# Moving the transposed activations of a two-layer decoder trunk to addresses that are multiples of 128 bytes

## The chip, the cores and the metric

The kernel runs on one core of one Trainium2 chip. The metric is the device time of one execution in microseconds (us). The kernel before took 676.93 us in the median of three runs (676.45 to 677.07).

## The reference

A causal decoder trunk of two layers over 256 tokens of 1024 features, all in float32. Each layer is a token mixer, a squared-ReLU MLP and a gated embedding; a final norm ends it.

```
u = rms_norm(h, attn_norm[i])
h = h + mixer_i(u)              # layer 0: 8 stick-breaking heads beside 4 differential heads
                                # layer 1: 16 heads of block attention (one block of 256 keys: causal softmax)
h = h + square(relu(rms_norm(h, mlp_norm[i]) @ w_ff1[i])) @ w_ff2[i]      # 1024 -> 4096 -> 1024
gate = sigmoid(rms_norm(h, ple_norm[i]) @ ple_gate[i])                    # 1024 -> 1024
h = h + gate * (p[i] @ ple_proj[i])                                       # 256 -> 1024
...
return rms_norm(h, final_norm)
```

The mixers project 1024 to 3072 features and the concatenated heads 1024 back to 1024.

## The kernel before

**Arithmetic.** To keep float32 accuracy at the speed of the one-pass format (float32r), each operand is split exactly into a high and a low part of that format, and each product is three matmuls into one bank of PSUM: high times high, high times low, low times high (`mm3`, and the same written out in `chunk_T` and `ff1`).

**Weights.** They stream from HBM in units of half a megabyte. A unit lands in one of four `raw` tiles; ScalarE writes its high part (`whi`, line 178) and VectorE the low part (`wlo`, line 192) into one of six pairs. TensorE releases a pair after its last product.

**Activations.** `transposes` turns the residual `h` with TensorE (line 170), ScalarE multiplies by the norm's gain from `gT`, and both parts go to one of two sets of transposed activations in turn: `T0h`/`T0l` and `T1h`/`T1l`, each tile [128, 8, 256] float32r, 8192 bytes in a partition. `Acts` hands the sets out by turns, so that the in-projections and the MLP's first product of both layers read `T0`, and the output projection of the mixer and the gate read `T1`. Attention results are written into `T1` by `average` and `put_T`.

**Which operand is which.** A matmul has a stationary operand, loaded into the array by LDWEIGHTS, and a moving one. The trace names them as bank<-moving,stationary. There are three kinds:
- `chunk`, `out_proj` and `gate`: 128 tokens of `T0` or `T1` are stationary, 512 columns of weights move (`bank<-whi,T0h` and so on). Only the last quarter of the last gate is cut to two pieces of 256 columns.
- `chunk_T` (line 574) and `ff1` (line 969): 128 columns of weights are stationary, 256 tokens of `T0` move (`bank<-T0h,whi`).
- `ff2` (line 993): 128 tokens of `hid`, the MLP's inner tile, are stationary, 512 columns of weights move (`bank<-whi,hid`). `hid` is a tile [128, 2, 4, 256] of the pool `zpool` (two buffers, shared with the attention's `z`), written by `hidden`.

All matmuls of these kinds are issued by line 159.

**Order of the work.** Tasks are Python generators with ranks; a list scheduler with its own clock estimates decides the order in which instructions are issued, once, at build time. It knows nothing of addresses. The feed-forward alternates `ff1(c + 1)` and `ff2(c)` over eight blocks of 512 inner features: 96 matmuls of 256 columns, then 48 of 512. Query and key projections leave `chunk` as a task that ScalarE scales, GpSimd rotates (`tt_pool`, line 196) and TensorE transposes; meanwhile TensorE goes on with the next products.

**Where tiles lie.** A pool places its tiles one behind the other in the order of their first allocation, each rounded up to 32 bytes; a tile of a name already allocated takes that name's place again. The pools `cst`, `zpool` and `vpool` follow one another. `cst` begins on a multiple of 128. Its large tiles are multiples of 128 bytes long; the small ones ahead of the transposed sets are these (`make_identity`'s tile is 512 bytes):

```
pexp = cst.tile([P, 2], F32, name="pexp")          # 8 bytes, takes 32
one = cst.tile([P, 1], F32, name="one")            # 4 bytes, takes 32
posi = cst.tile([P, 2], I32, name="posi")          # 8 bytes, takes 32
invf = cst.tile([P, 8], F32, name="invf")          # 32 bytes
gT = cst.tile([P, 48], F32, name="gT")             # 192 bytes
tsets = [[cst.tile([P, 8, 256], F32R, name=f"T{s}{w}") for w in ("h", "l")] for s in range(2)]
cc = cst.tile([P, 2, 2, 8], F32, name="cc")        # 128 bytes, and sn the same
```

In the program's list of addresses `whi0` is at byte 32896 of a partition (257 times 128; the other `whi` and `wlo` follow at steps of 4096), `T0h` at 131776 (1029 times 128, plus 64), `T0l`, `T1h` and `T1l` at steps of 8192 behind it, `pT` at 165856 (plus 96), and the two buffers of `hid` at 196224 and 204416 (1533 and 1597 times 128). All slices that the matmuls take of these tiles begin at multiples of 512 bytes in their tile.

Of the kernel before, what the change touches and what calls it, by code (L numbers as in the profile page):

```python
# [9 lines left out]
F32 = mybir.dt.float32  # L10
F32R = mybir.dt.float32r
# [6 lines left out]
P = 128  # L18
# [28 lines left out]

# ---- order of issue: tasks are generators that yield what they wait for; the one of the
# highest rank whose wait is over by the clocks of the engines issues next ----
class Event:  # L50
# [4 lines left out]
class Buffers:  # L55
    """Buffers that tasks take and give back."""

# [25 lines left out]
class Order:  # L83
# [65 lines left out]

    # -- instructions, each returning when its result can be read --  # L150
    def mm(self, out, lhsT, rhs, start, stop, **kw):
# [10 lines left out]
    def mm_halves(self, steps):  # L162
        """(out, lhsT, rhs, start, stop), 64 columns of the array each, two at a time side by side"""
        for out, lhsT, rhs, start, stop in steps:
            self.nc.tensor.matmul(out, lhsT, rhs, start=start, stop=stop)  # L165
            e = self.spend("pe", 0.84 * width(rhs) + 33)
        return e
# [13 lines left out]
    def after(self, out, *ins):  # L181
        """when the engine's own results are there"""
        w = 0.0
        for i in ins:
            if not isinstance(i, (int, float)) and i is not None:
                w = max(w, self.vis.get(i.tensor.name, 0.0))
        self.mine = out.tensor.name
        return w
# [24 lines left out]
    def copy(self, out, in_, ps=False, scale=None, dep=0.0):  # L213
        """On the engine that is through with it first."""
        n = width(out)
        ptr = scale is not None and not isinstance(scale, (int, float))
        ca = (52 if ps else 94) + 0.833 * n + (93 if ptr else 0)
        cv = 65 + (65 if ptr else 0) + (1.04 if ps else 0.52) * n
        if max(self.now, self.clk["act"], dep) + ca <= max(self.now, self.clk["dve"], dep) + cv:
            return self.act(out, in_, AF.Copy, ps=ps, dep=dep, scale=1.0 if scale is None else scale)  # L220
        if scale is None:
            self.nc.vector.tensor_copy(out, in_)
            return self.spend("dve", cv, dep)
        return self.ts(out, in_, scale, None, dep=dep, ps=ps)
# [3 lines left out]
def kernel(  # L228
# [7 lines left out]
    cst = ctx.enter_context(tc.tile_pool(name="cst", bufs=1))  # L236
# [5 lines left out]
    o = Order(nc)  # L242
# [14 lines left out]

# [1 line left out]
    h = [cst.tile([P, D], F32, name=f"h{t}") for t in range(2)]  # L259
# [34 lines left out]
    def constants_task():  # L294
# [4 lines left out]
        nc.gpsimd.memset(cmask, 0.0)  # L299
        # rows are queries, columns keys: a key after its query is out  # L300
        nc.gpsimd.affine_select(out=cmask[:, P:], in_=cmask[:, P:], pattern=[[-1, P]], base=0,
# [3 lines left out]
        for j in range(2):  # L305
            # rows are keys, columns queries: only keys before the query stay
            nc.gpsimd.affine_select(out=smask[:, j, :], in_=smask[:, j, :], pattern=[[1, P]], base=0,
                                    channel_multiplier=-1, compare_op=ALU.is_gt, fill=NEG)
        # negl[j, s] = -1 where j >= s
        nc.gpsimd.affine_select(out=neg[:, 0], in_=neg[:, 0], pattern=[[-1, P]], base=0,  # L310
# [17 lines left out]

    gT = cst.tile([P, 48], F32, name="gT")
    gT_ev = Event()  # L330
# [11 lines left out]

    o.add(gain_task(grow_a, 0, 16, 2800.0, gT_ev), 0)
    o.add(gain_task(grow_b, 16, 32, small_ev, Event()), 40)

# [1 line left out]
    specs = []  # L347
# [32 lines left out]
    units = []  # L380
# [33 lines left out]
    def short(eng, n):  # L414
        """at once when fewer than n units are ready, else when the engine is idle"""
        return lambda: o.now if ready[0] - used[0] < n else o.clk[eng]
# [41 lines left out]

# [1 line left out]
    tsets = [[cst.tile([P, 8, 256], F32R, name=f"T{s}{w}") for w in ("h", "l")] for s in range(2)]  # L460
    tnext = [0]
# [6 lines left out]

# [1 line left out]
    class Norm:  # L470
        """rs = 1/rms, rs8 = rs/8, rs2 = 1/rms^2 of each token tile"""

# [9 lines left out]
    def transposes(nm, t, c, dep, calm=False):  # L482
        """h[t][:, c] -> acts"""
        yield dep
# [27 lines left out]
    def statistics(nm, t, pieces, need):  # L512
        """pieces of the row: (first column, columns, event)"""
        for i, (c0, n, ev) in enumerate(pieces):
# [21 lines left out]

# [1 line left out]
    def mm3(ps, ahi, alo, whi, wlo, start, stop):  # L538
# [4 lines left out]
    def chunk(acts, sink, tmajor=False):  # L543
        """512 output features, token-major; sink(t, bank) is a task"""
        us = [take() for _ in range(4)]
# [28 lines left out]
    def chunk_T(acts, sink):  # L574
        """512 output features on partitions, 128 at a time; sink(f2, bank) is a task for two such blocks"""
        us = [take() for _ in range(4)]
# [15 lines left out]

# [1 line left out]
    cc = cst.tile([P, 2, 2, 8], F32, name="cc")  # L594
    sn = cst.tile([P, 2, 2, 8], F32, name="sn")
    rope_ev = Event()
# [42 lines left out]
    def rows_task(nm):  # L639
        """1/rms of each token along the columns, on every partition"""  # L640
        yield (nm.ev[0], nm.ev[1])
# [39 lines left out]
    def average(w0, w1, v, c0, acts, j, buf):  # L681
        """sum over keys of weights times values, for two heads of 64 features; w0(head) are the weights
        of the first 128 keys for all queries, w1(head) those of the last 128 for the last 128"""
        yield lambda: banks.wake(side=True)
# [12 lines left out]
    def put_T(oo, dep, acts, j):  # L697
        """token-major oo [128, 2 x 128] -> 128 features of acts"""
        yield dep
# [11 lines left out]

# [1 line left out]
    scores = [0, None]  # L713

    def scored():
        """a pair's scores are out"""
        scores[0] -= 1
        if scores[0] == 0:
            scores[1].t = o.now
# [45 lines left out]

# [1 line left out]
    def soft(j, t, qT, kz, q_ev, k_ev, e, st):  # L767
        """e [128, 2, (t+1)*128]; st: a column each for -max (2), sums (2), 1/sums (2)"""
        n = (t + 1) * P
# [9 lines left out]
        for g in range(2):  # L779
            # e = -(scores + mask), and its minimum is -max  # L780
            nc.vector.tensor_tensor_reduce(e[:, g, :], s3[:, g, :], cmask[:, P * (1 - t):], -1.0, 3.0e38, ALU.add, ALU.min,
                                           accum_out=st[:, g:g + 1])
            w = o.spend("dve", 130 + 1.04 * n)
# [63 lines left out]
    def moba_pair(j, jj, qT, kz, q_ev, k_ev, v, v_ev, acts):  # L847
        """heads 2*jj, 2*jj+1; j is the pair's place in its group"""
        yield (q_ev[0], k_ev[0], lambda: big.wake(2), lambda: tinies.wake(2))
# [25 lines left out]

# [1 line left out]
    def residual(t, c, bk, dep, scale, nm, h_ev):  # L877
# [186 lines left out]
    def finish(t, nm, gB, pieces):  # L1064
        """(h * gain) / rms, out"""
        parts = []
# [9 lines left out]

# [1 line left out]
    def table_task():  # L1078
# [12 lines left out]
        for t in range(2):  # L1091
            nc.gpsimd.tensor_tensor(ang[:, t, :], invf, posf[:, t:t + 1].to_broadcast([P, 8]), op=ALU.mult)  # L1092
        # ang = (ka 2^14 + kb) 2 pi + rem, with parts of 2 pi short enough that each product is exact
        magic, inv, b14 = 1.5 * 2.0 ** 23, 1.0 / (2.0 * math.pi), 2.0 ** 14
# [21 lines left out]
        yield e  # L1116
        # half angles: sin r = 2 sin(r/2) cos(r/2), cos r = 1 - 2 sin(r/2)^2
        o.act(sh, rem, AF.Sin, scale=0.5)
# [15 lines left out]
        rope_ev.t = e  # L1134
        # lambda of the differential heads, on every partition
        yield (28000.0, small_ev)
# [16 lines left out]
    o.add(table_task(), 15)  # L1153

    pT = cst.tile([P, 2, 2, 256], F32R, name="pT")

# [21 lines left out]
    def z_tile(name, layer, j):  # L1178
        """[128 features of two heads, pair, head, 256 tokens]; the other head's rows stay zero"""
        z = zpool.tile([P, 4, 2, 256], F32R, tag="z", name=name)  # L1180
# [11 lines left out]

# [1 line left out]
    def trunk():  # L1194
# [92 lines left out]
```

## Time and profile before

| | |
|---|---|
| median of three runs | 676.93 us (676.45 to 677.07) |
| profiled execution, first to last instruction | 674.7 us |
| TensorE matmul | 656.8 us busy, 97%, 3906 instructions |
| weight load (LDWEIGHTS) | 569.6 us, 84% |
| VectorE | 451.6 us, 67% |
| ScalarE | 417.1 us, 62% |
| GpSimd | 61.9 us, 9% |
| granted TensorE clock | 0.998 of full speed |
| DMA | 115.61 MB, 171 GB/s in the mean |

The profiled execution has a span of 674.7 us; the runs' median of 676.93 us has 2.2 us around such a span. Matmuls are pipelined: the recorded duration of one is longer than the distance from its start to the next one's start. That distance (the pitch below) is what the time is made of when TensorE never stops, and it is read from the starts in the timeline.

### The profile page before, as it was taken

What the parts mean: (1) busy time and instruction counts of PE and PEld (TensorE: products, weight loads), DVE (VectorE), ACT (ScalarE), POOL (GpSimd) and SP (SyncE); (2) the same over time, 40 slices, a digit from 0 to 9 for tenths busy, and PEclk for the clock granted to TensorE, in tenths of its full rate; (3) what the DMA queues carried; (4) which work ended last, traced back from release to release, by engine and by line L of the source; (5) the groups of instructions that cost most, each with busy time, mean ns of one, the idle gap of its engine ahead of it and who ended that gap; (6) DMA issues with size and microseconds to landing.
All of it is one profiled execution on the core that took longest, in us unless ns stands there. A gap on an engine that the chain in (4) does not pass through costs nothing.

```text
span 674.7 us, 10997 instructions
## 1 busy us (share of the span) xinstructions
PE 656.8 (97%) x3906; PEld 569.6 (84%) x3906; DVE 451.6 (67%) x936; ACT 417.1 (62%) x886; POOL 61.9 (9%) x129
## 2 busy tenths in 40 slices
PE   6799999999999999999999999999999999999995
PEld 4589878899998999898887777778998999899885
DVE  6789767777456554666895776758657545655584
ACT  7667887675446553655796776758646544655482
POOL 8820001000000000000043022000000000000010
PEclk9999999999999999999999999999999999999999
DMA  7753643456466546754656434435476546654621
GB/s 256 219 202 93 199 130 114 133 170 227 150 223 218 169 153 210 229 173 140 198 184 197 139 113 145 156 94 176 146 242 207 167 149 226 219 169 150 211 95 62
DMA packets 50054, 115.61 MB, mean 171 GB/s; under 512 B 4000, under 2 KB 5456, under 8 KB 50000
## 3 DMA queue, kind: packets, MB, share of 16 engines
q1 hardware_dynamic: 49824, 114.39, 52.0%
q8 instruction: 30, 0.49, 0.3%
q0 software_dynamic: 176, 0.53, 0.3%
q14 instruction: 24, 0.20, 0.1%
HBM read 113.86 MB, written 1.05 MB: 170 GB/s over the span
## 4 chain that ended last, share of the span: by engine, by line
PE 83%; issue 8%; POOL 7%; ACT 0%; DVE 0%; POOLq 0%; DVEq 0%; ACTq 0%
PE bank L159 80%; POOL rp L196 3%; PE bank L170 2%; PE bank L165 1%; POOL tok L196 1%; POOL prod L1102 1%; POOL rem L1103 1%; ACT tok L178 0%; POOL zl L1184 0%; POOL z L1185 0%; POOL z L1184 0%; POOL zl L1185 0%; POOL ang L1092 0%; POOL rs_a L527 0%; POOL rs_f L527 0%
## 5 line engine op out<-in xcount | busy, mean ns | idle before, releaser
L192 DVE TENSOR_TENSOR wlo<-raw,whi 128x512 fp32r<-128x512 f32 x424 | 276.9, 696 | 89.1 <-ACT whi L178 63.5
L178 ACT ACTIVATE whi<-raw 128x512 fp32r<-128x512 f32 x424 | 243.7, 628 | 97.9 <-PE bank L159 71.9
L159 PE MATMUL bank<-T0h,whi 128*128 128x256 f32 x576 | 161.7, 281 | 0.0
L159 PE MATMUL bank<-whi,hid 128*128 128x512 f32 x512 | 161.4, 391 | 0.0
L159 PE MATMUL bank<-T0l,whi 128*128 128x256 f32 x576 | 160.8, 279 | 0.0
L159 PE MATMUL bank<-T0h,wlo 128*128 128x256 f32 x576 | 160.7, 279 | 0.0
L159 PEld LDWEIGHTS bank<-whi,hid 128*128 128x128 f32 x512 | 96.1, 188 | 19.7
L159 PEld LDWEIGHTS bank<-T0h,whi 128*128 128x128 f32 x576 | 108.2, 188 | 0.7
L159 PEld LDWEIGHTS bank<-T0l,whi 128*128 128x128 f32 x576 | 107.8, 187 | 0.7
L159 PEld LDWEIGHTS bank<-T0h,wlo 128*128 128x128 f32 x576 | 108.2, 188 | 0.0
L159 PE MATMUL bank<-wlo,hid 128*128 128x512 f32 x256 | 99.6, 389 | 0.0
L192 DVE TENSOR_TENSOR tok<-tok 128x512 f32<-128x512 f32 x32 | 22.1, 690 | 67.1 <-ACT tok L178 67.1
L159 PE MATMUL bank<-whi,T0h 128*128 128x512 f32 x160 | 66.1, 413 | 0.2
L159 PE MATMUL bank<-wlo,T0h 128*128 128x512 f32 x160 | 63.7, 398 | 0.5 <-DVE wlo L192 0.4
L159 PE MATMUL bank<-whi,T0l 128*128 128x512 f32 x160 | 63.4, 396 | 0.0
L178 ACT ACTIVATE tok<-bank 128x512 f32<-128x512 f32 x32 | 18.8, 589 | 71.9 <-PE bank L159 71.9
L159 PEld LDWEIGHTS bank<-wlo,hid 128*128 128x128 f32 x256 | 48.1, 188 | 9.4
L159 PE MATMUL bank<-whi,T1h 128*128 128x512 f32 (+1 forms) x136 | 53.8, 396 | 0.0
L159 PE MATMUL bank<-whi,T1l 128*128 128x512 f32 (+1 forms) x136 | 51.8, 381 | 0.0
L159 PE MATMUL bank<-wlo,T1h 128*128 128x512 f32 (+1 forms) x136 | 51.8, 381 | 0.0
L527 POOL TENSOR_TENSOR rs_p<-ms_p,pexp 128x1 f32<-128x1 f32 x4 | 2.2, 552 | 436.0 <-DVE ms_p L209 436.0
L159 PEld LDWEIGHTS bank<-wlo,T0h 128*128 128x128 f32 x160 | 30.2, 189 | 7.7 <-DVE wlo L192 1.8
(161 smaller groups left out, 737.3 us busy)
## 6 DMA issues: line engine op xcount, KB each, us to landing
raw<-in_w_ff_dram SPq DMA_DIRECT2D x128, 512.0 KB, 4.4
raw<-in_moba_w_in_dram SPq DMA_DIRECT2D x24, 512.0 KB, 4.4
raw<-in_ab_w_in_dram SPq DMA_DIRECT2D x23, 512.0 KB, 4.7
raw<-in_ple_gate_dram SPq DMA_DIRECT2D x16, 512.0 KB, 4.7
raw<-in_ab_w_out_dram SPq DMA_DIRECT2D x8, 512.0 KB, 4.5
raw<-in_moba_w_out_dram SPq DMA_DIRECT2D x8, 512.0 KB, 3.3
raw<-in_ple_proj_dram SPq DMA_DIRECT2D x4, 512.0 KB, 3.3
h<-in_x_dram SPq DMA_DIRECT2D x4, 256.0 KB, 5.6
```

The source lines that it names most:

```text
L159: self.nc.tensor.matmul(out, lhsT, rhs, start=start, stop=stop, **kw)
L165: self.nc.tensor.matmul(out, lhsT, rhs, start=start, stop=stop)
L170: self.nc.tensor.transpose(out, in_, ident)
L178: self.nc.scalar.activation(out, in_, func, **kw)
L192: self.nc.vector.tensor_tensor(out, a, b, op=op)
L196: self.nc.gpsimd.tensor_tensor(out, a, b, op=op)
L527: nc.gpsimd.tensor_tensor(nm.rs[:, t:t + 1], b, pexp[:, 0:1], op=ALU.pow)
L1102: nc.gpsimd.tensor_scalar(prod, k, -c, None, op0=ALU.mult)
L1103: nc.gpsimd.tensor_tensor(dst, prod, src, op=ALU.add)
```

## The change

Only the allocation of small tiles in `cst` is changed; no instruction is added, removed or put elsewhere. `cc` (128 bytes) goes ahead of `T0h`, in the place of `gT`. Between `T0l` and `T1h` come `gT` (192), `sn` (128) and an unused tile of 64. Behind `T1l` comes another unused tile of 64. `gain_task` is added to the list of tasks a little later, with the same ranks. In `table_task`'s neighbourhood a tile named `room2` is allocated a second time. Comments and docstrings go as well (left out here).

```
-    gT = cst.tile([P, 48], F32, name="gT")
     gT_ev = Event()
...
-    o.add(gain_task(grow_a, 0, 16, 2800.0, gT_ev), 0)
-    o.add(gain_task(grow_b, 16, 32, small_ev, Event()), 40)
...
-    tsets = [[cst.tile([P, 8, 256], F32R, name=f"T{s}{w}") for w in ("h", "l")] for s in range(2)]
+    cc = cst.tile([P, 2, 2, 8], F32, name="cc")
+    tsets = [[cst.tile([P, 8, 256], F32R, name=f"T0{w}") for w in ("h", "l")]]
+    gT = cst.tile([P, 48], F32, name="gT")
+    sn = cst.tile([P, 2, 2, 8], F32, name="sn")
+    cst.tile([P, 16], F32, name="room")
+    tsets.append([cst.tile([P, 8, 256], F32R, name=f"T1{w}") for w in ("h", "l")])
+    cst.tile([P, 16], F32, name="room2")
+    o.add(gain_task(grow_a, 0, 16, 2800.0, gT_ev), 0)
+    o.add(gain_task(grow_b, 16, 32, small_ev, Event()), 40)
     tnext = [0]
...
-    cc = cst.tile([P, 2, 2, 8], F32, name="cc")
-    sn = cst.tile([P, 2, 2, 8], F32, name="sn")
...
     o.add(table_task(), 15)
 
+    cst.tile([P, 16], F32, name="room2")
     pT = cst.tile([P, 2, 2, 256], F32R, name="pT")
```

## Rows read from the trace of the kernel before

**Rows 1.** The page: busy us, share, instructions; granted clock in 40 slices.

```profile
PE 656.8 (97%) x3906; PEld 569.6 (84%) x3906; DVE 451.6 (67%) x936; ACT 417.1 (62%) x886; POOL 61.9 (9%) x129
PEclk9999999999999999999999999999999999999999
```

**Rows 2.** Busy time by stretch: us; PE PEld DVE ACT POOL; clock, DMA, GB/s.

```profile
136.00:312.40 176.40, 176.40 (x1148) 161.33 (x1147) 104.89 (x171) 93.25 (x170) 0.00 (x0) 1.00 0.58 192
...
462.60:639.10 176.50, 176.50 (x1149) 161.38 (x1148) 105.22 (x172) 93.57 (x170) 0.00 (x0) 1.00 0.58 192
```

**Rows 3.** The chain that ended last, in order of time: start, us, what.

```profile
43.41 0.46 POOL tok L196
...
135.91 176.49 PE bank L159 x1146
...
327.80 6.30 PE bank L159 x27
...
462.64 176.50 PE bank L159 x1146
```

**Rows 4.** Waits of PE: who for whom, us in total, times, longest.

```profile
PE bank L170 <- POOL tok L196: 3.0, 5, 1.3
```

**Rows 5.** PE's timeline in ff2: start us, us, what; every third is wlo.

```profile
300.21 0.39 PE L159 MATMUL bank<-wlo,hid 128*128 128x512 f32 x1
...
308.37 0.39 PE L159 MATMUL bank<-wlo,hid 128*128 128x512 f32 x1
```

**Rows 6.** PE's timeline in the last gate: the first and last of 48.

```profile
648.83 0.40 PE L159 MATMUL bank<-whi,T1l 128*128 128x512 f32 x1
...
659.79 0.39 PE L159 MATMUL bank<-wlo,T1h 128*128 128x512 f32 x1
```

**Rows 7.** Groups by shape: matmuls, count, busy us, mean ns, idle before.

```profile
L159 PE MATMUL bank<-T0h,whi 128*128 128x256 f32 x576 | 161.7, 281 | 0.0
L159 PE MATMUL bank<-whi,hid 128*128 128x512 f32 x512 | 161.4, 391 | 0.0
L159 PE MATMUL bank<-whi,T0l 128*128 128x512 f32 x160 | 63.4, 396 | 0.0
L159 PE MATMUL bank<-whi,T1l 128*128 128x512 f32 x120 | 47.4, 395 | 0.0
L159 PE MATMUL bank<-whi,T1h 128*128 128x256 f32 x16 | 4.4, 276 | 0.0
L159 PE MATMUL bank<-sph,negr 128*128 128x256 f32 x8 | 1.6, 278 | 0.0
```

**Rows 8.** PE's timeline in ff1: the first and last of 126.

```profile
146.09 0.28 PE L159 MATMUL bank<-T0l,whi 128*128 128x256 f32 x1
...
160.81 0.28 PE L159 MATMUL bank<-T0h,whi 128*128 128x256 f32 x1
```

**Rows 9.** PE's timeline at the last gate's end: the first and last of 48.

```profile
661.66 0.28 PE L159 MATMUL bank<-whi,T1h 128*128 128x256 f32 x1
...
666.99 0.28 PE L159 MATMUL bank<-whi,T1l 128*128 128x256 f32 x1
```

**Rows 10.** PE's timeline in chunk_T: the first and last of 33.

```profile
62.62 0.28 PE L159 MATMUL bank<-T0h,wlo 128*128 128x256 f32 x1
...
66.25 0.28 PE L159 MATMUL bank<-T0l,whi 128*128 128x256 f32 x1
```

**Rows 11.** PE's timeline in ff2 after four transposes: start us, us, what.

```profile
640.78 0.39 PE L159 MATMUL bank<-wlo,hid 128*128 128x512 f32 x1
...
641.71 0.62 PE L159 MATMUL bank<-whi,hid 128*128 128x512 f32 x2
...
642.85 0.39 PE L159 MATMUL bank<-wlo,hid 128*128 128x512 f32 x1
```

**Rows 12.** Groups by shape: weight loads, count, busy us, mean ns, idle before.

```profile
L159 PEld LDWEIGHTS bank<-whi,hid 128*128 128x128 f32 x512 | 96.1, 188 | 19.7
L159 PEld LDWEIGHTS bank<-whi,T0h 128*128 128x128 f32 x160 | 30.3, 189 | 7.4 <-DVE T0h L503 0.5 <-issue 0.5 <-ACT whi L178 0.5
```

## The prediction, made before the changed kernel was run

> **What bounds the kernel now.** I read the page first: TensorE's matmuls are busy 97% of the span and the granted clock is at full speed in every slice [rows 1], its level of 2.4 GHz. Busy time says little of a pipelined engine, so next comes the table by stretch: in the two feed-forward stretches TensorE is busy in all 176.4 and 176.5 us, while VectorE has 105, ScalarE 93 and DMA 0.58 of the time [rows 2]. The chain of waits agrees: both stretches are one piece of matmuls, 1146 in a row, with no releaser in it [rows 3]. There the time is the number of matmuls times their pitch, and only a shorter pitch or fewer matmuls help. Up to 43.9 us the chain runs over GpSimd's rotations instead (their last piece ends then, [rows 3]). Elsewhere TensorE waits for little: 3.0 us in five waits for a rotated tile [rows 4].
>
> So I read pitches in the timeline, and beside each the place of the operands. By the program's addresses all weights lie on multiples of 128 bytes.
> - 512 columns, `hid` stationary, on a multiple of 128: from 300.21 to 308.37 us are 36 matmuls, 226.7 ns each [rows 5].
> - 512 columns, `T1` stationary, 64 past a multiple: 47 pitches in 10.96 us, 233.2 ns [rows 6]. No transposes interrupt either stretch, and the moving tiles are the same. Only the stationary tile and its address differ. The mean durations say it for all of them: 391 ns against 396 and 395 [rows 7] (the `hid` group includes restarts, so 5 is a little low).
> - 256 columns, `T0` moving, 64 past: 125 pitches in 14.72 us, 117.8 ns [rows 8].
> - 256 columns of weights moving, on a multiple, `T1` stationary: 47 pitches in 5.33 us, 113.4 ns [rows 9].
>
> A slow class is thus 6.5 ns over its fast one at 512 columns and 4.4 ns at 256.
>
> **The change, part by part.** Addresses first. `pexp` and `one` take 64 bytes, `posi` and `invf` another 64, so `gT` began on a multiple of 128, and its 192 bytes put `T0` and `T1` 64 past. Now `cc` with 128 bytes is ahead of `T0`, and `gT`, `sn` and the spare (192 + 128 + 64 = 384) are between the sets: all four tiles lie on multiples. What follows moves by 128 in sum if the second `room2` takes the first one's place: `pT` stays 96 past, and `hid` goes from 196224 to 196352, from one multiple to the next. It was aligned already, so that half of the change moves nothing that rows 5 and 6 tell apart.
>
> *Term 1, `ff1`.* Two layers, eight blocks, 96 matmuls: 1536 of 256 columns with `T0` moving. No row shows this class with both operands on multiples in a long run. Bounds: no gain (117.8 stays), or 113.4 as in [rows 9], 4.4 × 1536 = 6.8 us. Nothing excludes a loss, but the eight short aligned ones `sph,negr` have a mean of 278 ns, between the 276 of a 113.4 pitch and the 281 of `T0h,whi` [rows 7]: no worse than now. I take 6.8, since rows 9 are the nearest in moving operand and width.
>
> *Term 2, `chunk_T`.* 192 of the same class; about 55 of them already run at the fast pitch (33 from 62.62 to 66.25 us: 3.63 us for 32 pitches, 113.4 [rows 10]). 137 × 4.4 = 0.6, of which I take 0.4, as transposes cut the stretch often. Bounds 0 and 0.6.
>
> *Term 3, `T0` and `T1` as stationary operand, 512 columns.* Groups of 160 and 120, three of each [rows 7]: 840 matmuls. The 96 of the first two projections come before 43.9 us, under the rotations, and gain nothing. 744 × 6.5 = 4.8 us is the most. But transposes cut these stretches, some 27 matmuls apart in [rows 3], and `hid`, aligned as it is, needs a start: after transposes the four pitches from 640.78 to 641.71 take 232.5 ns each, the five up to 642.85 228 [rows 11]. Six slow ones in 27 cost about a quarter: 3.6 us. Bounds 0 (the address of the stationary tile isn't the cause) and 4.8.
>
> *Term 4, what comes late next.* The rotations on GpSimd take as long as before, and the products that cover them get shorter. At each wait for a rotated tile [rows 4] the cover is some 5 us of 512-column products, which lose 3% or 0.15 us; three of the five waits are in the part that gains: 0.4 us given back. If the cover went at every transpose of the second layer's projections, all that term 3 gains there would go: 288 × 6.5 × 0.75 = 1.4 us.
>
> *Nothing.* Weights must arrive 2% faster in the feed-forward; DMA is at 0.58 there and VectorE has 71 us to spare [rows 2], and they would have to slow by a half to show. Writers of the moved tiles (ScalarE, VectorE) have the same cover. `gain_task` moves in the list, but no other task of its rank is ahead of it or behind it in a tie, so each queue keeps its order; no wait, transfer or instruction is added.
>
> Sum: 6.8 + 0.4 + 3.6 − 0.4 = 10.4 us off the profiled execution's 674.7, 664.3. The runs' median is 2.2 above that span, so 676.93 − 10.4 = **666.5 us**. If every restart ran at the fast pitch too, 12.2 less: 664.7.
>
> **Rivals.**
> *A, only the stationary operand's address counts.* For it: chunk_T reached 113.4 with `T0` still 64 past [rows 10], so a moving operand off its multiple doesn't by itself make the slow pitch; and the weights, stationary in `ff1`, are aligned already. Against: 1536 of 1536 in `ff1` look like [rows 8], and the one long run with aligned moving columns is fast [rows 9]. Terms 1 and 2 go: 3.6 − 0.4 = 3.2 off, 673.7.
>
> *B, no address counts; how a stretch starts decides its pitch.* For it: rows 8 and 10 are one class at one address with two pitches, and the loads themselves take 188 and 189 ns at either address [rows 12]. Against: `hid` falls into the fast pitch within about six matmuls even after transposes [rows 11], `T1` not in 47 [rows 6]. Time 676.9. The Trainium skill would side with it: the page "SBUF — State Buffer" (Specifications (TRN2)) gives SBUF lines of 16 bytes, and 64 is a multiple of 16, so 64 past and 0 past would be alike; "TensorE: Matmul & The Clock Gate" (Step-by-step: what each phase is for) gives the two operands independent read ports. By both the time would stay at 676.9; rows 5 and 6 differ by 6.5 ns with only the stationary tile exchanged, and disagree.
>
> *C, slower: the stationary tile must lie like the weights on a coarser grid.* The weights are at odd multiples of 128 (257 for `whi0`), and so was `hid` (1533); the change puts `hid` on an even one (1534), `T1h` too (148480 is 1160 times 128), `T0h` on an odd one (1029). If 256 bytes are the unit, `hid`'s 768 matmuls go to 233.2: 768 × 6.5 = +5.0; `T1` gains nothing; `T0` as stationary gains 384 × 6.5 × 0.75 = 1.9. With `ff1` unchanged that is +3.1, 680.0. It decides as long as `ff1` gains less than 2.0 ns a matmul (3.1 us over 1536); beyond that the kernel is faster even so, 673.2 with all of term 1. For it: no row has a stationary tile on the other half of 256, so nothing excludes it. Against: 64 past the grid and on it are all that the slow and fast classes show, and 128 is the smaller step that explains them.
>
> *D, the second `room2` takes 64 bytes of its own.* Then `hid` lies 64 past and pays 768 × 6.5 = 5.0: 671.5.
>
> **How the numbers follow.** Forecast 0.62, A 0.17, B 0.08, C 0.08 (slower), D 0.05. A measurement of this kernel tells some 0.2%, 1.4 us, from no change. Faster: forecast, A and D, 0.84; within: B, 0.08; slower: C, 0.08. The forecast's own range is 663.5 to 669; A's is 672.5 to 674.5. The range from 662.5 to 674 takes in the forecast, D and most of A, about 0.82.
>
> **What would show it.** The timeline of the changed kernel: `ff1` at 113.4 instead of 117.8 (mean duration near 276, not 280); matmuls with `T1` and `T0` stationary at 226.7 in long runs (means of 395 and 396 fall towards `hid`'s 391); `hid` still 226.7. The two feed-forward pieces of the chain would shrink by 3.4 us each. If `ff1` stays at 117.8, term 1 is wrong and A holds; if `T1` stays at 233, term 3 is; if `hid` shows 233, C or D, which the list of addresses tells apart. Waits of TensorE for rotated tiles above 3.5 us would show term 4 too small.

## The result, and the profile after

The changed kernel took 682.87 us in the median of four runs (682.60 to 683.07), the kernel before 676.71 us (676.45 to 677.07) beside it: a ratio of 1.0089, interval 1.0075 to 1.0103. It is slower by 0.9%; 666.5 us had been forecast, and the range ended at 674.

The page of the changed kernel, as [rows 1]: busy us, share, instructions; granted clock in 40 slices.

```profile
PE 664.3 (98%) x3906; PEld 576.2 (85%) x3906; DVE 451.4 (66%) x936; ACT 417.1 (61%) x886; POOL 62.6 (9%) x129
PEclk9899999999999999999999999999999999999999
```

TensorE is busy 7.5 us more with the same 3906 matmuls; VectorE and ScalarE have not changed. One slice is granted less than full clock: from 26 to 29 us the granted clock is 0.50, the lower of its two levels (1.2 GHz), just after TensorE had waited 1.8 us for GpSimd (in the kernel before it waited 1.6 us there, and the clock stayed). That lies under GpSimd's rotations, and the first 43.9 us take as long as before. Next, busy time by stretch of the changed kernel (us; PE, PEld, DVE, ACT, POOL; clock, DMA share, GB/s), cut where the feed-forward pieces begin and end:

```profile
0.00:43.90 43.90, 35.42 (x154) 27.30 (x154) 30.95 (x73) 29.96 (x68) 33.88 (x80) 0.96 0.75 239
43.90:136.20 92.30, 92.18 (x553) 78.67 (x554) 71.97 (x177) 68.20 (x162) 2.81 (x4) 1.00 0.43 135
136.20:316.10 179.90, 179.90 (x1149) 163.27 (x1148) 105.15 (x172) 93.48 (x170) 0.00 (x0) 1.00 0.57 188
316.10:465.40 149.30, 148.56 (x756) 119.69 (x754) 113.27 (x289) 111.50 (x267) 22.86 (x40) 1.00 0.46 149
465.40:645.30 179.90, 179.90 (x1148) 163.26 (x1148) 105.44 (x172) 93.72 (x170) 0.00 (x0) 1.00 0.58 188
645.30:681.00 35.70, 28.35 (x154) 24.02 (x152) 24.61 (x56) 20.24 (x51) 3.07 (x5) 0.95 0.21 74
```

And the stretch between the two feed-forwards in the kernel before, the only one that became shorter:

```profile
312.40:462.60 150.20, 149.65 (x755) 119.68 (x754) 113.13 (x289) 111.52 (x268) 22.26 (x40) 1.00 0.46 149
```

The two feed-forwards grew from 176.4 and 176.5 us [rows 2] to 179.9 each, 6.9 us together; the layer between them lost 0.9. At full clock and full occupation only the pitch can have grown. The chain of waits of the changed kernel (start, us, what), as [rows 3], and its waits for rotated tiles, as [rows 4]:

```profile
136.22 179.90 PE bank L159 x1146
...
465.39 179.90 PE bank L159 x1146
```

```profile
PE bank L170 <- POOL tok L196: 1.9, 5, 0.5
```

The chain is the same two pieces of 1146 matmuls, each 3.4 us longer, and the waits for GpSimd became shorter. No other wait of TensorE grew by more than 0.4 us. Now the pitches, in PE's timeline of the changed kernel (start us, us, what); the pairs are the ends of a stretch in `ff1`, in `ff2`, in a product with `T0` stationary, and in the last gate:

```profile
146.15 0.28 PE L159 MATMUL bank<-T0l,whi 128*128 128x256 f32 x1
...
160.79 0.28 PE L159 MATMUL bank<-T0h,whi 128*128 128x256 f32 x1
...
254.83 0.39 PE L159 MATMUL bank<-wlo,hid 128*128 128x512 f32 x1
...
263.19 0.40 PE L159 MATMUL bank<-wlo,hid 128*128 128x512 f32 x1
...
407.73 0.39 PE L159 MATMUL bank<-whi,T0l 128*128 128x512 f32 x1
...
411.81 0.39 PE L159 MATMUL bank<-whi,T0l 128*128 128x512 f32 x1
...
654.79 0.40 PE L159 MATMUL bank<-wlo,T1h 128*128 128x512 f32 x1
...
665.95 0.39 PE L159 MATMUL bank<-wlo,T1h 128*128 128x512 f32 x1
```

- `ff1`: 122 pitches in 14.64 us, 120.0 ns; before 117.8 [rows 8].
- `ff2`: 36 in 8.36 us, 232.2 ns; before 226.7 [rows 5].
- `T0` stationary: 18 in 4.08 us, 226.7 ns; its class had 233.2 in the mean before.
- `T1` stationary: 48 in 11.16 us, 232.5 ns; before 233.2 [rows 6].

The groups by shape of the changed kernel (count, busy us, mean ns, idle before) say it for all matmuls, as [rows 7]: `T0h,whi` from 281 to 284, `whi,hid` from 391 to 395, `T1l` still at 395. `T0l` has 397 only because its group holds the matmuls under the lower clock.

```profile
L159 PE MATMUL bank<-whi,hid 128*128 128x512 f32 x512 | 163.7, 395 | 0.0
L159 PE MATMUL bank<-T0h,whi 128*128 128x256 f32 x576 | 163.4, 284 | 0.0
L159 PE MATMUL bank<-whi,T0l 128*128 128x512 f32 x160 | 63.6, 397 | 0.0
L159 PE MATMUL bank<-whi,T1l 128*128 128x512 f32 x120 | 47.4, 395 | 0.0
```

After 43.9 us `T0l` alone, in the kernel before and in the changed one, falls from 395 to 391:

```profile
L159 PE MATMUL bank<-whi,T0l 128*128 128x512 f32 x128 | 50.5, 395 | 0.0
...
L159 PE MATMUL bank<-whi,T0l 128*128 128x512 f32 x128 | 50.1, 391 | 0.0
```

So `hid` and `ff1`, which moved from one multiple of 128 to the next or onto one, became slower; `T1`, moved onto one, gained nothing; `T0` as stationary operand gained what was forecast. The mean pitch of every class, from all its starts in both traces (pauses at transposes left out), gives the sum:

| class | count | before, ns | after, ns | us |
|---|---|---|---|---|
| `ff1`, `T0` moving, 256 columns | 1536 | 117.8 | 119.9 | +3.2 |
| `ff2`, `hid` stationary, 512 | 768 | 227.4 | 232.3 | +3.8 |
| `chunk_T`, 256 | 192 | 116.7 | 119.5 | +0.5 |
| `T0` stationary, 512, after 43.9 us | 384 | 233.2 | 228.4 | −1.8 |
| `T1` stationary, 512 | 360 | 233.2 | 232.5 | −0.3 |
| gate's end, 256 | 47 | 113.4 | 118.5 | +0.2 |
| sum | | | | +5.6 |

The spans differ by 6.4 us (674.7 and 681.1), the medians by 6.2. Start against start, in the same order of matmuls, 0.6 us of the 0.8 that the sum leaves lies between the matmuls of attention and the transposes, most of it in two gaps that grew by 0.26 and 0.22 us.

The program's addresses are now `T0h` 131712, `T1h` 148480, `hid` 196352; `whi0` stays at 32896 (128 past a multiple of 256). Below, the *distance* of a class is the address of its stationary tile less that of its moving tile, modulo 256. By the change it went from 0 to 128 in `ff2`, from 192 to 0 in `ff1`, from 64 to 0 with `T0` stationary, from 64 to 128 with `T1`.

### The profile page after: what moved, and what is told of

Its sections match the earlier page's. It is cut to its first block, busy times and chain, and to the rows that moved or that the text cites. A ratio compares the mean times of both kernels' runs of the same rounds, so it can differ in the third digit from the quotient of the medians.

```text
span 681.1 us, 10997 instructions
## 1 busy us (share of the span) xinstructions
PE 664.3 (98%) x3906; PEld 576.2 (85%) x3906; DVE 451.4 (66%) x936; ACT 417.1 (61%) x886; POOL 62.6 (9%) x129
## 4 chain that ended last, share of the span: by engine, by line
PE 79%; issue 9%; POOL 7%; ACT 2%; DMA 1%; DVE 1%; POOLq 0%; DVEq 0%; ACTq 0%
PE bank L159 76%; POOL rp L196 3%; PE bank L170 2%; POOL tok L196 1%; PE bank L165 1%; ACT tok L178 1%; DMA raw<-in_ab_w_out_dram 1%; POOL prod L1105 1%; DMA raw<-in_ab_w_in_dram 1%; POOL rem L1106 1%; ACT whi L178 1%; DVE wlo L192 0%; ACT junk L178 0%; POOL z L1189 0%; POOL zl L1188 0%
## 5 line engine op out<-in xcount | busy, mean ns | idle before, releaser
L159 PE MATMUL bank<-whi,hid 128*128 128x512 f32 x512 | 163.7, 395 | 0.0
L159 PE MATMUL bank<-T0h,whi 128*128 128x256 f32 x576 | 163.4, 284 | 0.0
L159 PE MATMUL bank<-T0h,wlo 128*128 128x256 f32 x576 | 163.0, 283 | 0.0
L159 PE MATMUL bank<-T0l,whi 128*128 128x256 f32 x576 | 162.9, 283 | 0.0
L159 PEld LDWEIGHTS bank<-T0h,whi 128*128 128x128 f32 x576 | 110.5, 192 | 0.8
L159 PEld LDWEIGHTS bank<-T0l,whi 128*128 128x128 f32 x576 | 110.5, 192 | 0.8
L159 PEld LDWEIGHTS bank<-T0h,wlo 128*128 128x128 f32 x576 | 110.5, 192 | 0.0
L159 PE MATMUL bank<-wlo,hid 128*128 128x512 f32 x256 | 101.0, 394 | 0.0
L159 PEld LDWEIGHTS bank<-whi,T0l 128*128 128x128 f32 x160 | 30.7, 192 | 6.6
```

## The experiments

The theory (R in the expectations): a pitch depends on the distance alone, whichever tiles are multiplied and wherever both lie. Its rivals: each tile's own address counts; the unit is another than 256; nothing but the way a stretch is entered counts. "Spare" in an edit is a tile that nothing uses.

**e1: `hid` alone back to distance 0**, one multiple of 256 from where it was before.

```
 # the allocations of after, behind zl
+    cst.tile([P, 32], F32, name="padc_128")       # hid 196352 -> 196480
```

> The changed kernel with 128 unused bytes more behind zl, so that hid goes from 196352 to 196480: from an even multiple of 128 to an odd one, as the weights are, but 256 away from where it stood before. T0 and T1 stay as changed. Theory R (the pitch of a matmul depends on the distance between the places of its stationary and its moving tile, modulo 256 bytes): hid is in step with the weights again, its 768 matmuls go from 232.3 to 227.8 ns, 3.5 us less than the changed kernel, about 679.3 us. If the unit is 512 bytes: hid stays at 232 ns and the time at 682.9. Theory S (nothing is decided by addresses, each stretch falls into one of two pitches by how it starts): hid near 232, 682.9.

Measured: 679.18 us (679.08 to 679.68), 1.0039 of before (1.0025 to 1.0053). The timeline of e1 in `ff2`, 21 pitches in 4.76 us, 226.7 ns:

```profile
164.08 0.39 PE L159 MATMUL bank<-wlo,hid 128*128 128x512 f32 x1
...
168.84 0.39 PE L159 MATMUL bank<-wlo,hid 128*128 128x512 f32 x1
```

128 unused bytes take back 3.7 us of the loss. Since 196480 is 256 from the place before, a unit of 512 bytes is out for this class, and since 128 and 0 differ in pitch, so is one of 128: it is 256.

**e2: `T0` alone moved**, as in the change; `T1` and `hid` where they were.

```
-    gT = cst.tile([P, 48], F32, name="gT")        # in front
...
+    cc = cst.tile([P, 2, 2, 8], F32, name="cc")
+    tsets = [[... "T0h", "T0l"]]
+    ang = cst.tile([P, 2, 8], F32, name="ang")
+    tsets.append([... "T1h", "T1l"])
+    gT = ...; ka = ...                            # and sn behind zl
```

> The kernel before with T0 alone moved by 64 bytes to where the change puts it (131712, 128 modulo 256, in step with the weights); T1, hid and everything behind stay where they were before. Theory R: ff1 goes from 117.8 to 120.0 ns as in the changed kernel (1536 x 2.2 = 3.4 us, chunk_T 0.5 us more), T0 as stationary operand goes from 233 to 228 (384 x 5 = 1.9 us less), hid stays at 227.8 and T1 at 233: 676.8 + 2.0 = 678.8 us. Rival (T0 as moving operand is better on a multiple, and ff1 is slow in the changed kernel for what hid or T1 do around it): ff1 at 117.8 or below, 675 us or less.

Measured: 678.67 us (678.55 to 679.05), 1.003 (1.0019 to 1.0041). Mean pitches: `ff1` 119.9, `T0` stationary 228.2, `hid` 227.3, `T1` 233.2. The groups by shape of e2:

```profile
L159 PE MATMUL bank<-T0h,whi 128*128 128x256 f32 x576 | 163.5, 284 | 0.0
...
L159 PE MATMUL bank<-wlo,hid 128*128 128x512 f32 x256 | 99.8, 390 | 0.0
...
L159 PE MATMUL bank<-whi,T1l 128*128 128x512 f32 x120 | 47.4, 395 | 0.0
```

So putting `T0` on a multiple of 128, by itself, loses: `ff1` pays 3.2 us for it and `chunk_T` 0.6, and the stationary side earns 1.9. This is Term 1 tested alone, with the opposite sign. Together with e1 the loss is in its two parts, `hid` 3.7 and `T0` 2.0; 0.5 of the 6.2 belongs to neither.

**e3: every tile 64 bytes further**, so that no tile has the address modulo 256 that it had, and all distances stay.

```
 # before, ahead of all tiles of cst
+    cst.tile([P, 16], F32, name="pada_64")
```

> The kernel before with 64 unused bytes ahead of all tiles: every tile moves by 64, so all distances between tiles stay. Theory R: all pitches and the time as before (hid 227.8, T0 and T1 233 as stationary, ff1 117.8), 676.8 us. Rival (a tile's own address counts, whatever it is used with): hid leaves its multiple of 128 and goes to 233, +4 us; T0 and T1 reach a multiple of 256 and change too, ff1 between 113 and 120: time off by 2 us or more either way.

Measured: 676.47 us (676.43 to 677.08), 0.9999 (0.999 to 1.0008). The groups by shape of e3 answer to [rows 7]; `T0l` has 401 for 396, as e3 too has a granted clock of 0.50 from 26.3 to 29.7 us, and its pitch after that keeps its mean of 233.2:

```profile
L159 PE MATMUL bank<-T0h,whi 128*128 128x256 f32 x576 | 161.7, 281 | 0.0
...
L159 PE MATMUL bank<-wlo,hid 128*128 128x512 f32 x256 | 99.6, 389 | 0.0
...
L159 PE MATMUL bank<-whi,T0l 128*128 128x512 f32 x160 | 64.1, 401 | 0.0
...
L159 PE MATMUL bank<-whi,T1l 128*128 128x512 f32 x120 | 47.4, 395 | 0.0
```

The time does not change when all weights lie 64 past a multiple of 128, and the one fast stretch of `chunk_T` [rows 10] stays the only one. So whether a tile itself lies on a multiple of 128 counts for nothing. Shifts of less than 64 bytes for all tiles were not tried.

**e4: each class at the best distance then known**: 64 in `ff1`, 0 for `T1` and `hid`, 192 for `T0` as stationary.

```
 # before; gT no longer in front
+    ang = cst.tile([P, 2, 8], F32, name="ang")    # T0h at 131648
+    tsets = [[... "T0h", "T0l"]]
+    ka = cst.tile([P, 2, 8], F32, name="ka")      # T1h at 148096
+    tsets.append([... "T1h", "T1l"])
+    gT = ...; sn = ...                            # and cc behind zl
```

> T0 at 131648 (64 modulo 256), T1 at 148096 (128 modulo 256), hid and all behind where they were before. In ff1 the stationary weights are then 64 ahead of the moving T0, the distance that the last 256-column products of the gate had before (weights moving, T1 stationary 64 ahead: 113.4 ns). Theory R: ff1 at 113.4 (1536 x 4.4 = 6.8 us less than before), T1 at 228 (360 x 5 = 1.8 less), hid 227.8; T0 as stationary operand is then 64 behind the weights, a distance not seen yet, 226 to 233 (0 to 2 less): 676.8 - 8.6 to 10.5, about 667.5 us. Rival (113.4 was a matter of how that stretch was entered, as in chunk_T before): ff1 stays near 118, only T1 gains, 675 us.

Measured: 672.42 us (672.03 to 672.61), 0.9937 (0.9924 to 0.9949): faster than before, and 4.9 us short of what was expected. The timeline of e4 in two blocks of `ff1`:

```profile
145.82 0.28 PE L159 MATMUL bank<-T0h,whi 128*128 128x256 f32 x1
...
159.99 0.28 PE L159 MATMUL bank<-T0h,wlo 128*128 128x256 f32 x1
...
171.00 0.28 PE L159 MATMUL bank<-T0h,whi 128*128 128x256 f32 x1
...
182.18 0.28 PE L159 MATMUL bank<-T0h,wlo 128*128 128x256 f32 x1
```

The first pair spans 125 pitches of 113.4 ns, the second 95 of 117.7. So there are two pitches at one distance, 64, and R does not hold for 256 columns. The 192 matmuls with which each layer's feed-forward begins are fast; the six blocks entered from `ff2` stay slow for all of their 96. The 12 slow blocks hold 1152 matmuls: 1152 × 4.4 = 5.1 us, the miss.

**e5 to e8: four more distances**, each run once, beside one run of the kernel before at 676.85 us. The four move `T0`, `T1` and `hid` in the way of e4 with spares of 32 to 224 bytes. Their distances are, for `T0` as stationary, `T0` as moving (`ff1`), `T1` and `hid`: e5 128, 128, 192, 192; e6 32, 224, 224, 32; e7 224, 32, 96, 224; e8 96, 160, 160, 96.

> One look at three distances from the weights at once (a tile's place less the weights' place, modulo 256; the weights are at 128): T0 at 128, T1 at -64, hid at -64. Theory R: each class keeps one pitch for one distance wherever it occurs: ff1 with T0 at 128 like the 256-column tail of the gate with T1 at 128 in the changed kernel, 118.5 ns; T1 and hid as stationary at -64 like T0 in the run before, 229 to 230 ns; T0 as stationary at 128 like hid and T1 in the changed kernel, 232.3. Against the kernel before: ff1 +1.1, hid +1.7, T1 -1.3, about 678 us. Rival (the nearer a multiple of 256 the better): hid at -64 as bad as +64, 233, and ff1 at 120: 682 us.

> One look: T0 at a distance of +32 from the weights, T1 at -32, hid at +32. Theory R with a unit of 64 bytes inside the 256: a tile at +32 reaches over two units at once, so its pitch lies between that of 0 and of +64: hid and T0 as stationary 227 to 233 (230), T1 at -32 227 to 230, ff1 between 117.8 and 120 (119). Against the kernel before: ff1 +1.8, hid +1.8, T0 -1.1, T1 -1.5: 678 us. Rival (only the remainder by 64 counts beside the distance): all three in the slow class, 233 and 118, 680 us.

> One look: T0 at -32, T1 at +96, hid at -32. Theory R: hid and T0 as stationary between 0 and -64, 227 to 230; T1 at +96 like pT, 233; ff1 with T0 at -32, that is the stationary weights 32 ahead, between 120 and the mixture of 113.4 and 117.8 that -64 gave, 117 to 119. 677 us. Rival: as in the run at +32, 680 us.

> One look: T0 at +96, T1 at -96, hid at +96. Theory R: hid and T0 as stationary like pT, which is at +96 in the kernel before: 233.3; T1 at -96 between -64 and 128, 230 to 232; ff1 with T0 at +96 between 117.8 (+64) and 118.5 (128). Against the kernel before: hid +4.2, ff1 +0.5, T1 -0.7: 681 us. Rival (a start off a multiple of 64 costs by itself): hid above 234 and ff1 above 120, 684 us or more.

Measured: 680.28, 679.4, 682.52 and 686.11 us. All four are slower than R expected, since the unknown distances were taken too low; e6 and e8 came nearer to their rivals (680, and 684 or more). e5 also misses in kind: R had `ff1` at distance 128 like the gate's end of the changed kernel, 118.5 ns. The timeline of e5 in `chunk_T` and in `ff1`, both at distance 128:

```profile
51.06 0.28 PE L159 MATMUL bank<-T0h,whi 128*128 128x256 f32 x1
...
54.86 0.28 PE L159 MATMUL bank<-T0h,wlo 128*128 128x256 f32 x1
...
146.74 0.28 PE L159 MATMUL bank<-T0h,whi 128*128 128x256 f32 x1
...
160.66 0.28 PE L159 MATMUL bank<-T0h,wlo 128*128 128x256 f32 x1
```

The first pair spans 32 pitches of 118.8 ns, the second 116 of 120.0. All runs together give a table of pitches (ns; the means of classes, or, where one distance has two pitches, those of its long stretches):

| distance | 512 columns | 256 columns |
|---|---|---|
| 0 | 226.8–227.4 (`hid`), 228.2–229.1 (`T0`, `T1`, cut by transposes) | 119.5–119.9 |
| 32 | 233.1–233.3 | 118.3 |
| 64 | 233.2 | 113.4 or 117.8 |
| 96 | 233.4–234.1 | 118.6 |
| 128 | 232.3–232.7 | 118.5–118.8 or 120.0 |
| 160 | 233.2 | 119.8–120.0 |
| 192 | 228.9–230.0 | 113.4 or 117.8 |
| 224 | 232.1–233.2 | 116.7–116.9 |

Each line holds more than one pair of tiles. At 512 columns 64 has `T0` and `T1` of before and `hid` of e10. At 256 columns the line for 0 holds `ff1` of the changed kernel (`T0` moving, weights stationary) and the gate's end in e4, where the roles are exchanged. At 192 `ff1` of the kernel before has 117.8 [rows 8] and one stretch of `chunk_T` 113.4 [rows 10]. At 512 columns the classes at one distance lie within 2.5 ns of one another; at 256 columns there are two pitches at 64, 128 and 192. Multiples of 128 do not sort the lines: 128 is slow at 512 columns, and the slowest is e8 with `hid` at 96, 21 pitches in 4.92 us, 234.3 ns. The timeline of e8 in `ff2`:

```profile
163.91 0.40 PE L159 MATMUL bank<-wlo,hid 128*128 128x512 f32 x1
...
168.83 0.40 PE L159 MATMUL bank<-wlo,hid 128*128 128x512 f32 x1
```

**e9 and e10: what is `ff1` entered from?** If the stretch before it decides, another pitch of `ff2` should change `ff1`, although `ff1`'s own distance stays 64.

```
 # e4, behind cc
+    cst.tile([P, 48], F32, name="padz_192")       # e9: hid at distance 192
+    cst.tile([P, 16], F32, name="padz_64")        # e10 instead: hid at distance 64
```

> The best guess so far (T0 64 behind the weights, T1 in step) with 192 unused bytes behind zl, so that hid goes from a distance of 0 to one of 192 from the weights. In the run with hid at 0 the 1536 matmuls of ff1 were fast (113.4 ns) in the two first blocks of each layer, which are not entered from ff2, and slow (117.8) in all blocks entered from ff2. Theory E (at this distance both pitches hold themselves, and ff2 with hid in step hands over the slow one): with hid out of step ff1 is entered fast, 1152 x 4.4 = 5.1 us less; hid at 192 costs 768 x 2.3 = 1.8 more: 672.4 - 3.3 = 669.1 us. Rival (the slow pitch comes from the place in the program, any entry from ff2 brings it): ff1 as before, only the cost of hid: 674.2 us.

> The same with hid at a distance of 64 (192 modulo 256, where T1 was before: its last 512-column products at 233 ns handed over 113.4 to the 256-column ones). Theory E: ff1 fast in all blocks, 5.1 us less; hid at 64 costs 768 x 6.4 = 4.9 more: 672.4 - 0.2 = 672.2 us. Rival: ff1 as before, 677.3 us.

Measured: e9 668.8 us (668.62 to 669.03), 0.9883 (0.9867 to 0.9898); e10 674.8 (674.5 to 675.11), 0.9972 (0.9961 to 0.9983). The timeline of e9 in the block that was slow in e4:

```profile
171.26 0.28 PE L159 MATMUL bank<-T0h,wlo 128*128 128x256 f32 x1
...
181.46 0.28 PE L159 MATMUL bank<-T0h,wlo 128*128 128x256 f32 x1
```

90 pitches in 10.20 us, 113.3 ns: every block of e9 that follows `ff2` is fast from its sixth matmul on. `hid` itself pays for that with 228.9 instead of 226.8 ns, 768 × 2.1 = 1.6 us, and `ff1` gains 1536 × (116.7 − 113.5) = 4.9. The timeline of e10, in that block and the next:

```profile
171.18 0.28 PE L159 MATMUL bank<-T0h,whi 128*128 128x256 f32 x1
...
182.37 0.28 PE L159 MATMUL bank<-T0h,wlo 128*128 128x256 f32 x1
...
193.69 0.28 PE L159 MATMUL bank<-T0h,whi 128*128 128x256 f32 x1
...
204.47 0.28 PE L159 MATMUL bank<-T0h,wlo 128*128 128x256 f32 x1
```

95 pitches each, 117.8 and 113.5 ns: in e10 the blocks alternate, and its time lies between the two expected, 672.2 and 677.3. So `hid`, which `ff1` does not read, decides with its place which of the two pitches `ff1` takes at distance 64; and since in e4 the blocks that do not follow `ff2` are fast, the stretch before a block is the likely way. The pitch of `ff2` alone does not decide it, since e10's blocks alternate although each is entered from an `ff2` at the same distance. e9 is the fastest of all the versions, 1.2% below the kernel before and 2.1% below the changed one (668.8 / 682.87). The chain of waits of e9, pieces of 173.8 us where [rows 3] have 176.5:

```profile
135.27 173.78 PE bank L159 x1146
...
457.86 173.78 PE bank L159 x1146
```

## Why the prediction was wrong, step by step

**What bounds the kernel** held: 5.6 of the 6.4 us are in the pitch of matmuls that follow one another without a stop, and no other engine or transfer is seen to have a part in it.

**The failed step** came before the terms: "all weights lie on multiples of 128 bytes", and then one address was read from each row, that of the tile that the change moved. In [rows 5, 6] only the stationary tile differs, so its own multiple looked like the cause; but the two also differ in their distance to the weights, 0 and 64, and no row told the two readings apart. e3 does: with every tile moved by 64 the pitches and the time stay. And e1 does: `hid` lies on a multiple of 128 at 196352 and at 196480, and its pitch is 232.3 at the one and 227.3 at the other.

**Term 1** (6.8 us off, measured 3.2 on) was sized from [rows 9], "the nearest in moving operand and width". That row has distance 64, and the change put `ff1` at 0, which no long row of before showed at 256 columns. The bound that was named and not taken, "nothing excludes a loss", was the right one; its eight short matmuls spoke too weakly. [Rows 9] themselves went from 113.4 to 118.5 when their distance went to 128.

**"That half of the change moves nothing that rows 5 and 6 tell apart"**, of `hid`, was the larger mistake: put at nothing, it measured +3.8 us. e1 undoes it with 128 bytes.

**Term 2** fails as term 1 does: +0.5 for −0.4. The fast stretch around [rows 10] is 45 matmuls long in the trace, not about 55.

**Term 3** came true for `T0`, now at the distance that `hid` had: 384 × 4.8 = 1.8 of its part of the 3.6. `T1` at 128 gained 0.3 where about 1.8 were counted. The mean of 228.4 in place of 226.7 agrees with the cost counted for restarts.

**Term 4** was not seen: PE's waits for rotated tiles are 1.9 us in place of 3.0.

**The rivals.** A falls with `hid` and `ff1`; B with e1, where one spare tile changes 768 pitches. But its mechanism, that how a stretch starts decides, has e4, e9 and e10 for it at distance 64. It may also be why [rows 8, 10], both at 192, have two pitches in one class; no run tested that. D is out: `hid` is at 196352, a multiple of 128, so the second `room2` took no bytes of its own. C, held at 0.08, came nearest: 256 is the unit, `hid` loses and `T1` gains nothing, as it said (680.0). It asked only where the stationary tile lies and left `ff1` unchanged; with `ff1`'s +3.2 its sum is 683.2, 0.3 from the measurement. The argument against it, that "128 is the smaller step that explains them", was a preference and not a row.

**Open.** Why the distance matters is only argued: the next stationary tile is loaded while the moving one streams (664 us of matmuls and 576 of loads in a span of 681), so that both are read from one partition at once, and some distances might make the reads collide. No run here looks into that. Nor is it shown what picks the pitch where one distance has two, or why e10 alternates (the two buffers of `hid` take turns in the same rhythm, and no run separates the two). The weights were never moved by anything but 64, so for the distances that are not multiples of 64 (e6 to e8) a tile's own address and its distance are not told apart. The sum by classes leaves 0.8 us of the 6.4, of which only the place is known.

## What to carry to other kernels

Where TensorE runs without a stop, list for each class of matmuls the address of the stationary tile less that of the moving one, and compare pitches by that difference; a tile that serves as both has two of them, and what helps one role can cost the other. Before a class is moved to a place that no long row shows, try it with one spare tile: here the places of small tiles and of 96 to 192 unused bytes made the kernel up to 1.4% slower (e8) and up to 1.2% faster (e9). When two rows seem to isolate a cause, ask what else differs between them by the same amount.

## What was not expected of the hardware

- The pitch of a 512-column product went from 226.8 to 234.1 ns, and of a 256-column one from 113.4 to 120.0, over the distances tried, with nothing but the places of tiles changed; the granted clock was at full speed in all these stretches.
- The best distance differs by width: 0 at 512 columns (226.8), 64 at 256 (113.4, where the fast one of its two pitches is taken), while 0 is among the worst at 256 (119.9).
- One class at one distance has two pitches, 113.4 and 117.8 ns, each kept for a whole block of 96 matmuls (e4, e10); moving `hid`, the stationary tile of the products before it, changes which one is taken (e9).
